# Seven half-depth products for 18 of the 52 pairs of weight chunks in a two-layer hybrid attention trunk

## The chip, the cores and the metric

The kernel runs on one core of one Trainium2 chip. The metric is device time in microseconds; lower is better. Five engines work side by side, each in the order of its own instruction queue: PE multiplies matrices, DVE (VectorE), ACT (ScalarE) and POOL (GpSimd) work elementwise, and SP only starts transfers. ACT and POOL have queues for transfers as well. On-chip memory is SBUF; PE writes its results to eight banks of PSUM.

## The reference

Two layers work on x of 256 tokens by 2048 channels, all in float32. Each layer does this:

```python
h = rms_norm(x, norm_gain)
proj = jnp.einsum('bsd,de->bse', h, w_in)          # 2048 -> 20480, ten segments of 2048
(da_q, da_k, da_v, da_z, sb_q, sb_k, sb_v, sb_z, gate_a, gate_b) = split_columns(proj)
...                                                # da_q, da_k: rms_norm per head, rope
oa = differential_attention(...)                   # softmax(q1 k1) - lam * softmax(q2 k2), times v
ua = rms_norm(oa, subln_gain) * (1.0 - lambda_init) * silu(da_z)
ub = stick_breaking_attention(qs, ks, vs) * silu(sb_z)
y = sigmoid(gate_a) * (ua @ w_branch_a) + sigmoid(gate_b) * (ub @ w_branch_b)
x = x + y @ w_out
```

So a layer multiplies 256 tokens with thirteen weight matrices of 2048 by 2048: ten segments of w_in, two branch projections and one output projection. Both attentions are causal, with 128-token query blocks.

## The kernel before

A **chunk** is 512 columns of such a matrix, so each matrix has four chunks and a layer has 52; the two layers together have 52 pairs of chunks. A chunk arrives from DRAM as eight tiles of 128 x 1024 float32 (512 KB): each holds two of its 16 depth tiles of 128 rows.

PE takes its operands in a reduced float32 format. To keep precision, each operand is split in two: a high part `h` (ACT copies it into the reduced format) and a rest `l` (DVE subtracts `h` from the source). `split` in L61 and L62 does that for every weight tile (`wraw` into `wh` and `wl`) and for every activation. `mm3` in L65 to L67 then adds three matmuls into one PSUM bank: high by high, high by rest, rest by high. Each has 512 columns for a weight chunk.

`project` multiplies one chunk: for eight weight tiles, two depth tiles each, two token tiles and three matmuls, 96 matmuls in all, into two of the four PSUM banks of the pool `ps_mm`. With four banks, the next chunk can start while the last one is still being read out. `load_w` loads a weight tile on SP's queue (four `wraw` buffers) and splits it (three buffers each for `wh` and `wl`).

A layer goes through four groups of differential attention and then four of stick-breaking attention. A group is four chunks (q, k, v, z) with the attention of its heads: `da_qk` normalises per head and applies rope (squares on ACT, the root by `rsqrt_mean` on POOL, the rest on DVE and POOL), `put_T` transposes on PE and splits, `scores` and `attn_T` make the weights, `v_proj` and `act_proj` read their PSUM banks with the scale of the layer's input norm. That scale is applied after the projection: x goes in only multiplied by `norm_gain`, transposed (from the host for layer 0), and each result is multiplied with 1/rms of its token. So the first projection can begin while the sums of squares are still being made.

The branch results `ua` and `ub` stay in SBUF, split. In the merge, the gates are projected, then `w_a` from `ua` and `w_b` from `ub`; then the output projection follows. In layer 0, each finished output chunk is stored, multiplied with the next gain, transposed and split for layer 1.

The text of the program is not the order of the engines: a scheduler that plans with priorities (weight splits are raised by 400) arranges each engine's queue when the kernel is built. Buffers are handed out from pools; an instruction that needs a taken buffer waits for its last reader.

Of the kernel before, what the change touches and what calls it, by code (L numbers as in the profile page):

```python
# [9 lines left out]
F32 = mybir.dt.float32  # L10
# [22 lines left out]
QK_SCALE = HD ** -0.5  # L33

# [4 lines left out]
def trunk(ctx: ExitStack, tc: tile.TileContext, x, xT, gT, norm_gain, w_in, qk_gain, lam_vecs,  # L39
# [19 lines left out]

    def split(h, l, src):  # L60
        nc.scalar.copy(h, src)  # L61
        nc.vector.tensor_tensor(out=l, in0=src, in1=h.bitcast(F32), op=ALU.subtract)  # L62

    def mm3(ps, lh, ll, rh, rl, start, stop):
        nc.tensor.matmul(ps, lhsT=lh, rhs=rh, start=start, stop=False)  # L65
        nc.tensor.matmul(ps, lhsT=lh, rhs=rl, start=False, stop=False)  # L66
        nc.tensor.matmul(ps, lhsT=ll, rhs=rh, start=False, stop=stop)  # L67
# [5 lines left out]
    gcol = const.tile([P, KT], F32, name="gcol")  # L73
    nc.scalar.dma_start(out=gcol, in_=gT)

    def load_w(src, parts=1, between=None):
        raw = wp.tile([P, KK * CW], F32, name="wraw", bufs=4)
        h = wp.tile([P, KK * CW], F32R, name="wh")
        l = wp.tile([P, KK * CW], F32R, name="wl")
        n = KK * CW // parts  # L80
        for i in range(parts):
            c = slice(i * n, (i + 1) * n)
            nc.sync.dma_start(out=raw[:, c], in_=src[:, c])  # L83
            if between is not None and i == 0:
                between()
            with tc.high_priority(offset=400):
                split(h[:, c], l[:, c], raw[:, c])
        return h, l

    def project(src, lhs, before=None):  # L90
        ps = [ps_mm.tile([P, CW], F32, name="mm") for _ in range(NT)]
        for kp in range(KP):
            if before is not None and kp == 0:
                h, l = load_w(src[kp], KK, lambda: before(0))
            else:
                if before is not None:
                    before(kp)
                h, l = load_w(src[kp])
# [8 lines left out]
        return ps  # L107

    def pair(tag):
        return (big.tile([P, KT, S], F32R, name=tag + "h", tag=tag + "h"),  # L110
                big.tile([P, KT, S], F32R, name=tag + "l", tag=tag + "l"))

    def put_T(src, dst, c, t):
        """Four 128x128 blocks of src, transposed and split, into k-tiles 4c.. of dst."""
        tr = ps_tr.tile([P, CW], F32, name="tr")
# [4 lines left out]
        trv = heads(tr)  # L120
        split(dst[0][:, js, ts], dst[1][:, js, ts], trv)

    def rsqrt_mean(ss, n):
        """(ss / n + eps) ** -0.5"""
# [7 lines left out]

# [1 line left out]
    xt = pair("xT")  # L134
    ss_part = small.tile([P, NT, NG], F32, name="ss_part", bufs=2)
    sq_junk = const.tile([P, CW], F32, name="sq_junk")

    def first_input(kp):
        raw = work.tile([P, CW], F32, name="tok")
        if kp:  # L140
            nc.sync.dma_start(out=raw, in_=xT[:, kp * CW:(kp + 1) * CW])  # L141
        for j in range(KK):
            k = kp * KK + j
            rv = raw[:, j * S:(j + 1) * S]
            if kp:
# [36 lines left out]
    for l in range(DEPTH):  # L182
# [303 lines left out]
        if not last:  # L486
            xt = xt_n
            x_in = x_next
# [50 lines left out]
```

## Time and profile before

| what | value |
|---|---|
| median of three runs | 2439.18 us (2438.13 to 2440.94) |
| span of the profiled execution | 2436.2 us |
| PE busy | 2427.0 us, 11328 matmuls and transposes |
| DVE busy | 1430.3 us |
| ACT busy | 1257.7 us |
| POOL busy | 179.7 us |
| DMA, mean over the span | 186 GB/s, 453 MB |
| clock granted to PE | full, all through |

The profiled execution's span is 3.0 us below the median of the runs. In rows that list groups of instructions, the name to the left of `<-` is the tile that is written, those to the right are read; then come the shapes, the count, the busy time in us and the mean length of one instruction in ns, and last the idle time ahead of it with the engine that ended it. A matmul's length in such a row includes its way through the array; the next one starts earlier, so its cost in a stream is the distance between starts. The same holds, less strongly, for DVE. In the rows of a timeline the first number is the start in us from the beginning of the span, the second the length.

### The profile page before, as it was taken

What the parts mean: (1) busy time and instruction counts of PE and PEld (TensorE: products, weight loads), DVE (VectorE), ACT (ScalarE), POOL (GpSimd) and SP (SyncE); (2) the same over time, 40 slices, a digit from 0 to 9 for tenths busy, and PEclk for the clock granted to TensorE, in tenths of its full rate; (3) what the DMA queues carried; (4) which work ended last, traced back from release to release, by engine and by line L of the source; (5) the groups of instructions that cost most, each with busy time, mean ns of one, the idle gap of its engine ahead of it and who ended that gap; (6) DMA issues with size and microseconds to landing.
All of it is one profiled execution on the core that took longest, in us unless ns stands there. A gap on an engine that the chain in (4) does not pass through costs nothing.

```text
span 2436.2 us, 29977 instructions
## 1 busy us (share of the span) xinstructions
PE 2427.0 (100%) x11328; PEld 2019.4 (83%) x11328; DVE 1430.3 (59%) x1636; ACT 1257.7 (52%) x1771; POOL 179.7 (7%) x183
## 2 busy tenths in 40 slices
PE   9999999999999999999999999999999999999999
PEld 7888888888888888888888888888888888888887
DVE  7676766655656444555566757656556564445554
ACT  6555655645645444444455555556556454444443
POOL 2031130000000000000030321300000000000000
PEclk9999999999999999999999999999999999999999
DMA  8555555555555555556755555555555555555565
GB/s 291 170 174 179 173 179 179 175 176 171 172 179 174 196 191 195 191 192 201 240 199 173 176 179 173 173 182 173 173 174 173 182 173 192 196 191 191 189 206 182
DMA packets 128386, 453.39 MB, mean 186 GB/s; under 512 B 14321, under 2 KB 15089, under 8 KB 128241
## 3 DMA queue, kind: packets, MB, share of 16 engines
q1 hardware_dynamic: 127312, 449.24, 55.5%
q8 instruction: 89, 1.46, 0.3%
q0 software_dynamic: 640, 2.10, 0.2%
q14 instruction: 57, 0.46, 0.1%
q10 hardware_dynamic: 288, 0.14, 0.0%
HBM read 447.23 MB, written 4.19 MB: 185 GB/s over the span
## 4 chain that ended last, share of the span: by engine, by line
PE 99%; DMA 0%; SPq 0%; DVE 0%; ACT 0%; issue 0%; DVEq 0%
PE mm L66 31%; PE mm L67 31%; PE mm L65 31%; PE tr L117 2%; PE sc L67 1%; PE sc L66 1%; PE sc L65 1%; PE tr L323 1%; PE tr L415 0%; DMA wraw<-in_w_in 0%; DVE wl L62 0%; ACT wh L61 0%; SPq L148 0%; SPq L83 0%; SPq L141 0%; DVE tok L473 0%
## 5 line engine op out<-in xcount | busy, mean ns | idle before, releaser
L62 DVE TENSOR_TENSOR wl<-wraw,wh 128x1024 fp32r<-128x1024 f32 (+1 forms) x833 | 1026.3, 1232 | 838.1 <-ACT wh L61 837.5
L61 ACT CAST wh<-wraw 128x1024 fp32r<-128x1024 f32 (+1 forms) x833 | 875.7, 1051 | 969.8 <-PE mm L67 946.0
L66 PE MATMUL mm<-wl,xTh 128*128 128x512 f32 x2560 | 1004.6, 392 | 0.5 <-DVE wl L62 0.5
L67 PE MATMUL mm<-wh,xTl 128*128 128x512 f32 x2560 | 1004.6, 392 | 0.0
L65 PE MATMUL mm<-wh,xTh 128*128 128x512 f32 x2560 | 930.4, 392 | 4.6 <-DVE xTh L149 4.4
L65 PEld LDWEIGHTS mm<-wh,xTh 128*128 128x128 f32 x2560 | 480.5, 188 | 101.7 <-ACT wh L61 5.3
L66 PEld LDWEIGHTS mm<-wl,xTh 128*128 128x128 f32 x2560 | 481.5, 188 | 96.7 <-DVE wl L62 1.1
L67 PEld LDWEIGHTS mm<-wh,xTl 128*128 128x128 f32 x2560 | 481.5, 188 | 95.4
L66 PE MATMUL mm<-wl,uah 128*128 128x512 f32 x512 | 199.6, 390 | 0.0
L67 PE MATMUL mm<-wh,ual 128*128 128x512 f32 x512 | 199.3, 389 | 0.0
L65 PE MATMUL mm<-wh,uah 128*128 128x512 f32 x512 | 180.1, 390 | 0.0
L65 PEld LDWEIGHTS mm<-wh,uah 128*128 128x128 f32 x512 | 96.1, 188 | 19.9
L67 PEld LDWEIGHTS mm<-wh,ual 128*128 128x128 f32 x512 | 96.1, 188 | 19.8
L66 PEld LDWEIGHTS mm<-wl,uah 128*128 128x128 f32 x512 | 96.1, 188 | 19.7
L66 PE MATMUL mm<-wl,ubh 128*128 128x512 f32 x256 | 99.6, 389 | 0.0
L67 PE MATMUL mm<-wh,ubl 128*128 128x512 f32 x256 | 99.6, 389 | 0.0
L65 PE MATMUL mm<-wh,ubh 128*128 128x512 f32 x256 | 89.2, 389 | 0.0
L480 POOL DMA_DIRECT2D x_next<-tok x8 | 4.5, 567 | 828.8 <-DVE tok L473 828.8
L127 POOL TENSOR_SCALAR rv<-ssq 128x4 f32<-128x4 f32 (+1 forms) x48 | 26.7, 556 | 523.7 <-ACT sq_junk L372 272.5
L117 PEld LDWEIGHTS tr<-ident,tok 128*128 128x128 f32 x416 | 51.2, 140 | 12.5
L117 PE MATMUL tr<-ident,tok 128*128 128x128 f32 x416 | 60.9, 272 | 0.0
L130 POOL TENSOR_TENSOR rr<-rv,mhalf 128x4 f32<-128x4 f32 (+1 forms) x50 | 57.9, 1157 | 4.2
(115 smaller groups left out, 1524.8 us busy)
## 6 DMA issues: line engine op xcount, KB each, us to landing
wraw<-in_w_in SPq DMA_DIRECT2D x639, 512.0 KB, 3.3
wraw<-in_w_a SPq DMA_DIRECT2D x64, 512.0 KB, 3.3
wraw<-in_w_b SPq DMA_DIRECT2D x64, 512.0 KB, 3.3
wraw<-in_w_o SPq DMA_DIRECT2D x64, 512.0 KB, 3.9
tok<-in_x SPq DMA_DIRECT2D x8, 256.0 KB, 6.8
xr<-in_x SPq DMA_DIRECT2D x4, 512.0 KB, 5.6
x_next<-tok POOLq DMA_DIRECT2D x8, 256.0 KB, 5.2
xr<-x_next SPq DMA_DIRECT2D x4, 512.0 KB, 5.4
```

Of the source, the lines that this page charges most:

```text
L61: nc.scalar.copy(h, src)
L62: nc.vector.tensor_tensor(out=l, in0=src, in1=h.bitcast(F32), op=ALU.subtract)
L65: nc.tensor.matmul(ps, lhsT=lh, rhs=rh, start=start, stop=False)
L66: nc.tensor.matmul(ps, lhsT=lh, rhs=rl, start=False, stop=False)
L67: nc.tensor.matmul(ps, lhsT=ll, rhs=rh, start=False, stop=stop)
L117: nc.tensor.transpose(out=tr[:, j * P:(j + 1) * P], in_=src[:, j * P:(j + 1) * P], identity=ident)
L127: nc.gpsimd.tensor_scalar(out=v[:, :w], in0=ss, scalar1=1.0 / n, scalar2=RMS_EPS, op0=ALU.mult, op1=ALU.add)
L130: nc.gpsimd.tensor_tensor(out=r[:, :w], in0=v[:, :w], in1=mhalf[:, :w], op=ALU.pow)
L323: nc.tensor.transpose(out=tr[:, j:j + P], in_=a[:, j:j + P], identity=ident)
L480: nc.gpsimd.dma_start(out=x_next[t * P:(t + 1) * P, cs], in_=xn)
```

## The change

**Seven products.** Two weight chunks with the same left-hand side, side by side, form a right-hand matrix of 2048 by 1024. Cut in halves both ways, it has the blocks b11, b21 (the upper and lower half of the first chunk's depth) and b12, b22 (of the second chunk's). The left-hand side (the 256 normalised tokens) has four blocks as well: two token tiles by two halves of the depth. The eight block products become seven, in Winograd's arrangement of Strassen's method, each of half the depth (8 depth tiles) for one token tile: 7 x 8 x 3 = 168 matmuls, where two chunks took 192. `s_stream` does this. Four sums of left-hand blocks (`sm`, made and split once per layer by `left_sums`) replace some left-hand blocks; sums of right-hand blocks are made in place in the raw tiles. These sums are of three kinds: "a" adds b12 to b11, "c" adds b12 to the remainder, "d" adds b21; all three are transfers from DRAM that POOL issues and that add to what lies in SBUF (`accum_op=ALU.add`). "b" adds two raw tiles on DVE. In the gate pair "d" is also done on DVE, so that there are 12 such transfers in 16 of the pairs and 8 in two. Each of the 28 right-hand tiles of the seven products is split anew. The four result tiles come from five combinations on DVE, which read PSUM and held copies (`pp`, three of them made by ACT).

In each layer the pairs are v and z of all eight groups, and the second chunks of the two gates: 9 pairs per layer, 18 in all. All other chunks are multiplied as before (`c_stream`). `run` interleaves two such streams by their share of steps: beside a group's seven products go the q and k chunks of the next group, each followed by two empty steps (`GAP`).

**PSUM.** Two banks for `c_stream` (`mc`), three for the seven products (`sU`, `sN`, `sQ`), three for transposes, scores and attention results (`at`). Where no seven products run, successive chunks take turns between `mc` and `sU`/`sN`.

**Input normalised first.** x is loaded, squared, scaled with 1/rms and the gain, transposed and split before the first projection of a layer, in both layers (`normalised`). The scaling of the results disappears from the read-out.

**Branches in DRAM.** Each group's `ua` or `ub` part goes to DRAM (`spill`, on POOL's queue) and comes back before the merge (`reload`), since the sums `sm` take its place in SBUF. Raw tiles have ten buffers instead of four.

```diff
+RAW = 10
+PPB = 5
+GAP = 2
...
-    ps_mm = ctx.enter_context(tc.tile_pool(name="ps_mm", bufs=4, space=PSUM))
-    ps_tr = ctx.enter_context(tc.tile_pool(name="ps_tr", bufs=2, space=PSUM))
-    ps_sc = ctx.enter_context(tc.tile_pool(name="ps_sc", bufs=2, space=PSUM))
+    ps_c = ctx.enter_context(tc.tile_pool(name="ps_c", bufs=2, space=PSUM))
+    ps_s = ctx.enter_context(tc.tile_pool(name="ps_s", bufs=1, space=PSUM))
+    ps_at = ctx.enter_context(tc.tile_pool(name="ps_at", bufs=3, space=PSUM))
...
+        def add(dst, src, dma_src, key):
+            with tc.high_priority(offset=400):
+                if key in by_dma:
+                    nc.gpsimd.dma_start(out=dst, in_=dma_src, accum_op=ALU.add)
+                else:
+                    nc.vector.tensor_tensor(out=dst, in0=dst, in1=src, op=ALU.add)
+
+        def prod(ps, lhs, get, after=None, more=False):
+            for i in range(hk):
+                raw = get(i)
+                h, l = split_raw(raw)
+                for kk in range(KK):
+                    k = i * KK + kk
+                    cs = slice(kk * CW, (kk + 1) * CW)
+                    mm3(ps, lhs[0][:, k], lhs[1][:, k], h[:, cs], l[:, cs],
+                        k == 0 and not more, k == KT // 2 - 1, more)
+                if after is not None:
+                    after(i)
+                if i < hk - 1:
+                    yield
...
+        u_ps = ps_s.tile([P, CW], F32, name="sU")
+        yield from prod(u_ps, a(0, 0), loader(xs, b11), lambda i: add(xs[i], None, b12[i], "a"))
+        p1 = held("p1")
+        nc.scalar.copy(p1, u_ps)
+        yield
+
+        n_ps = ps_s.tile([P, CW], F32, name="sN")
+        yield from prod(n_ps, s(3), loader(zs, b22))
+        yield
+
+
+        def after5(i):
+            add(xs[i], zs[i], b22[i], "b")
+            add(zs[i], None, b12[i], "c")
+
+        q_ps = ps_s.tile([P, CW], F32, name="sQ")
+        yield from prod(q_ps, s(0), lambda i: xs[i], after5)
+        p5 = held("p5")
+        nc.scalar.copy(p5, q_ps)
+        yield
+
+        yield from prod(u_ps, s(1), lambda i: xs[i],
+                        (lambda i: add(xs[i], None, b21[i], "d")) if "d" in by_dma else None, True)
+        w = held("w")
+        nc.vector.tensor_tensor(out=w, in0=u_ps, in1=p5, op=ALU.subtract)
+        u = held("u")
+        nc.scalar.copy(u, u_ps)
+        fin(1, 0, lambda dst: nc.vector.tensor_tensor(out=dst, in0=n_ps, in1=w, op=ALU.subtract))
...
+        v_ps = ps_s.tile([P, CW], F32, name="sQ")
+        yield from prod(v_ps, s(2), lambda i: zs[i])
...
+        r_ps = ps_s.tile([P, CW], F32, name="sN")
+        yield from prod(r_ps, a(1, 0), loader(ws, b21),
+                        None if "d" in by_dma else (lambda i: add(xs[i], ws[i], None, "d")))
...
+        yield from prod(v_ps, a(1, 1), lambda i: xs[i], None, True)
...
+            s = s_stream(w_chunk(bases[0], g), w_chunk(bases[1], g), xt, sm,
+                         lambda col, t, op: cols[col](t, op), "acd")
+            if n + 1 < 2 * NG:
+                c = qk_streams(n + 1, gap=GAP)
...
+            run((2 * (C_STEPS + GAP), c), (S_STEPS, s))
...
+            nc.gpsimd.dma_start(out=xk[c], in_=x_in[:, cs].rearrange("(t p) d -> p t d", p=P))
+            run((1, c_stream([w_o[l, c, kp] for kp in range(KP)], yT, o_fin(c), c % 2 == 1)))
         if not last:
-            xt = xt_n
+            xt = normalised(xk, gb, ss_part)
```

How this moves the queues shows at three places.

On PE, in a differential-attention group of layer 0 before, where one chunk ends (banks 904 and 905) and the next begins (banks 1071 and 1072), without anything between:

```order
L65 MATMUL mm_905<-wh_1033,xTh_87 128x512
L66 MATMUL mm_905<-wl_1034,xTh_87 128x512
L67 MATMUL mm_905<-wh_1033,xTl_88 128x512
L65 MATMUL mm_1071<-wh_1074,xTh_87 128x512
L66 MATMUL mm_1071<-wl_1075,xTh_87 128x512
```

The same engine in the change, where a q chunk ends (bank 815 is its second token tile): transposes and scores (`at`) follow, then matmuls of the third product (`sQ`).

```order
L74 MATMUL mc_815<-wh_1059,xTl_132 128x512
L458 MATMUL at_766<-ident_85,tok_763 128x128 x2
L72 MATMUL at_771<-kTh_589,qTh_391 128x256
L73 MATMUL at_771<-kTl_590,qTh_391 128x256
L74 MATMUL at_771<-kTh_589,qTl_392 128x256
```

The k chunk's first matmul (`mc_1186`) comes 45 rows later, after the rest of the third product and the whole fourth.

On POOL, before, in the first differential-attention group: root (`rv`, `rr`) and rope (`tok`) of the k chunk.

```order
L127 TENSOR_SCALAR rv<-ssq 128x4
L130 TENSOR_TENSOR rr<-rv,mhalf 128x4
L260 TENSOR_TENSOR tok<-tok,t_k 128x4x64
L262 TENSOR_TENSOR tok<-tok,t_k 128x4x64
L127 TENSOR_SCALAR rv<-ssq 128x4
```

The change, at the same place, with the accumulating transfers into raw tiles between them:

```order
L141 DMA raw<-in_w_in 128x1024
L247 TENSOR_SCALAR rv<-ssq 128x4
L250 TENSOR_TENSOR rr<-rv,mhalf 128x4
L141 DMA raw<-in_w_in 128x1024
L404 TENSOR_TENSOR tok<-tok,t_k 128x4x64
L406 TENSOR_TENSOR tok<-tok,t_k 128x4x64
```

The second root of the chunk now stands behind transfers that wait for DVE's split of their tile.

On DVE, in a differential-attention group before, at the read-out of a q chunk (`mm`) with rope behind it:

```order
L62 TENSOR_TENSOR wl<-wraw,wh 128x1024 x6
L246 TENSOR_SCALAR cf<-rr,rstd_s 128x4
L250 TENSOR_TENSOR tok<-mm,cf 128x512
L62 TENSOR_TENSOR wl<-wraw,wh 128x1024
L257 TENSOR_TENSOR tok<-tok,t_q 128x512
L264 TENSOR_TENSOR tok<-tok 128x512
```

In the change, during the third product: "b" additions (L143) and softmax steps between the splits.

```order
L68 TENSOR_TENSOR wl<-raw,wh 128x1024
L143 TENSOR_TENSOR raw<-raw 128x1024
L480 RECIPROCAL rs<-sums 128x2
L68 TENSOR_TENSOR wl<-raw,wh 128x1024
L482 TENSOR_SCALAR nrs<-rs,nlam 128x2
L68 TENSOR_TENSOR wl<-raw,wh 128x1024
L143 TENSOR_TENSOR raw<-raw 128x1024
```

Where splits stood in runs of up to six, each split at this place is now followed by another DVE instruction.

More of the change, by code (lines that the diff above doesn't have):

```diff
@@ new lines, in trunk, with run, chain, slot @@
+    C_STEPS, S_STEPS = KP, 7 * KP // 2
+    def run(*streams):
+        live = [[n, 0, g] for n, g in streams]
+        while live:
+            s = min(live, key=lambda s: (s[1] + 0.5) / s[0])
+            if next(s[2], "end") == "end":
+                live.remove(s)
+            s[1] += 1
+    def chain(*gens):
+        for g in gens:
+            yield from g
+    def slot(tag, name):
+        return (big.tile([P, KT, S], F32R, name=name + "h", tag=tag + "h"),
+                big.tile([P, KT, S], F32R, name=name + "l", tag=tag + "l"))
@@ L169, in trunk @@
     nc.gpsimd.memset(mhalf, -0.5)
+    ss_part = small.tile([P, NT, NG], F32, name="ss_part", bufs=2)
+    xk = []
+    for c in range(NG):
+        xc = chunk_tile(c, "xk")
+        for t in range(NT):
+            nc.sync.dma_start(out=xc[:, t], in_=x[t * P:(t + 1) * P, c * CW:(c + 1) * CW])
+        xk.append(xc)
+    gb = gains(0)
+    for c in range(NG):
+        for t in range(NT):
+            squares(xk, c, t, ss_part)
+    xt = normalised(xk, gb, ss_part)
     masks = {}
```

525 lines of the change are left out of this document (310 added, 215 removed).

## The prediction

> **What bounds the kernel now.** I read the page's totals first, then the chain that ended last, then the busy time by stage.
>
> ```profile
> PE 2427.0 (100%) x11328; PEld 2019.4 (83%) x11328; DVE 1430.3 (59%) x1636; ACT 1257.7 (52%) x1771; POOL 179.7 (7%) x183
> PE 99%; DMA 0%; SPq 0%; DVE 0%; ACT 0%; issue 0%; DVEq 0%
> 0.00:45.00 45.00, 39.84 (x164) 32.04 (x165) 30.79 (x51) 32.64 (x65) 7.83 (x19) 1.00 0.91 328
> 45.00:330.00 285.00, 285.00 (x1361) 237.59 (x1360) 196.06 (x257) 162.00 (x308) 65.31 (x62) 1.00 0.53 175
> 420.00:800.00 380.00, 380.00 (x1834) 317.71 (x1833) 219.16 (x245) 211.43 (x255) 0.00 (x0) 1.00 0.53 175
> 840.00:1020.00 180.00, 180.00 (x800) 149.10 (x799) 87.96 (x78) 75.94 (x78) 0.00 (x0) 1.00 0.57 193
> ```
>
> The chain is PE from end to end. In the windows (start:end, length, then busy PE, PEld, DVE, ACT, POOL, then clock, DMA share, GB/s) PE is idle only at the start. 45 to 330 us holds three differential-attention groups, 95.0 us each, with DVE busy 65.4 us in each (69%); 420 to 800 us holds four stick-breaking groups, again 95.0 us, DVE 54.8 us. So matmuls taken away are worth their full spacing, until DVE, which splits every weight tile, or the DMA queues become the limit.
>
> **What the change takes away.** A pair of chunks is 192 matmuls of 512 columns; the seven products need 7 x 8 x 3 = 168. Eighteen pairs save 432.
>
> ```profile
> 118.04 0.39 PE L67 MATMUL mm<-wh,xTl 128*128 128x512 f32 x1
> 122.57 0.39 PE L67 MATMUL mm<-wh,xTl 128*128 128x512 f32 x1
> ```
>
> Between these two starts lie 20 spacings: 0.2265 us each. 432 x 0.2265 = **-97.8 us**. Shapes and operand types stay, so I keep the spacing. A group loses 24 matmuls: 95.0 - 5.4 = 89.6 us of PE.
>
> **What it adds on PE.** Layer 0's input is now transposed on the chip, 32 transposes.
>
> ```profile
> 1002.75 1.04 PE L117 MATMUL tr<-ident,tok 128*128 128x128 f32 x8
> 1003.54 0.48 PE L66 MATMUL mm<-wl,xTh 128*128 128x512 f32 x1
> ```
>
> Eight take 0.79 us up to the next start, 32 take **+3**.
>
> **Start.** Normalising first puts the whole of x, eight squares, the root and one transposed tile ahead of the first projection.
>
> ```profile
> 4.43 1.19 PE L65 MATMUL mm<-wh,xTh 128*128 128x512 f32 x2 [4.43 <-DVE xTh L149]
> tok<-in_x SPq DMA_DIRECT2D x8, 256.0 KB, 6.8
> L484 ACT ACTIVATE sq_junk<-tok 128x512 f32<-128x512 f32 x8 | 5.0, 628 | 0.1
> L484 ACT ACTIVATION_READ_ACCUMULATOR sq_junk<-tok 128x1 f32 x8 | 1.5, 186 | 0.0
> L130 POOL TENSOR_TENSOR rr<-rv,mhalf 128x2 f32<-128x2 f32 x18 | 12.6, 699 | 1.5
> L482 DVE TENSOR_TENSOR tok<-tok 128x512 f32<-128x512 f32 x8 | 5.5, 688 | 0.1
> L61 ACT CAST xTh<-tr 128x512 fp32r<-128x512 f32 x8 | 4.7, 583 | 3.8 <-PE tr L117 3.8
> ```
>
> Eight loads of 256 KB at the 328 GB/s of the first window take 6.4 us; with 3 us ahead of the first byte's use they are in at about 10. The last square ends 0.8 us later, reduction and root take 1.3 with hand-overs, then scale 0.69, transposes 0.4, cast 0.58: first matmul near 14 us. Today's start loses 45 - 164 x 0.2265 = 7.9 us, so +6. Then DVE is short: from the new order, with the spacing found below, the first 45 us of PE work carry 50 us of DVE work (splits, scaling, rope, the four left-hand sums). +4. Together **+10** (from 5, if DVE gets ahead while PE waits, to 16).
>
> **Layer boundary.** Before, the next layer's tiles were transposed chunk by chunk under the output projection. Now PE waits from the last output matmul through add 0.69, square 0.81, root 1.0, scale 0.69, transposes 0.4, cast 0.58, by the same rows: 4.2 and some 0.8 of hand-overs, then the same DVE shortage of 4. **+9** (5 to 14).
>
> **The splits.** Seven products split 28 right-hand tiles where 16 were split: 12 more casts on ACT, 12 more subtractions on DVE per pair, and four additions of 128x1024 on DVE.
>
> ```profile
> 142.39 1.22 DVE L62 TENSOR_TENSOR wl<-wraw,wh 128x1024 fp32r<-128x1024 f32 x1
> 143.52 0.68 DVE L62 TENSOR_TENSOR qTl<-tr,qTh 128x512 fp32r<-128x512 f32 x1
> 144.12 1.22 DVE L62 TENSOR_TENSOR wl<-wraw,wh 128x1024 fp32r<-128x1024 f32 x1
> 137.66 1.76 DVE L62 TENSOR_TENSOR wl<-wraw,wh 128x1024 fp32r<-128x1024 f32 x1
> 138.29 1.72 POOL L262 TENSOR_TENSOR tok<-tok,t_q 128x256 f32<-128x256 f32 x1
> ```
>
> Back to back, 1024 columns occupy DVE 1.13 us and 512 columns 0.60. So a group gains 16 x 1.13 + five combinations x 0.60 - four small cf operations x 0.23 = 20.2 us of DVE: 65.4 becomes 85.6 of 89.6 in differential attention (96%), 54.8 becomes about 76 in stick-breaking (85%). The gate pairs have almost only splits, 44 x 1.13 + 8 x 1.13 + 3 = 62 us beside 82. ACT gains 12 casts and copies, about 15 us on 54: no limit.
>
> PE need not wait by the sum alone. But DVE runs in order, only three wl buffers let it work ahead, and rope and softmax steps come in clusters. The last two rows show a subtraction stretched from 1.22 to 1.76 us while POOL ran beside it; 14 more POOL transfers per group (12 accumulating, 2 storing), each stretching one, would add 14 x 0.54 = 7.6 us: 93.2 against 89.6, and at 95% of DVE filled 98 us. So a differential-attention group costs between 0 and 8.4 us of waiting; nothing in the rows excludes either, and I take the middle, 4. The other ten stages lie between 0 (85% or less, as PE today meets 69% with no wait) and 3 (7.6 us more would bring 76 to 84 of 89.6); 1. 8 x 4 + 10 x 1 = **+42**.
>
> The Trainium skill, page "SBUF — State Buffer", section "Who interferes with whom", says that a DVE instruction with two SBUF inputs and a GpSimd instruction that reads SBUF exclude each other; the 1.76 us row agrees. [...]
>
> **One PSUM pair for the attention chunks.** With two banks instead of four, the next q or k chunk waits until the last is read out.
>
> ```profile
> 124.58 0.37 ACT L241 ACTIVATE sq_junk<-mm,rstd 128x128 f32<-128x128 f32 x1 [0.53 <-PE mm L67]
> 129.72 0.69 DVE L250 TENSOR_TENSOR tok<-mm,cf 128x512 f32<-128x512 f32 x1
> 136.32 0.69 DVE L250 TENSOR_TENSOR tok<-mm,cf 128x512 f32<-128x512 f32 x1
> ```
>
> From the first square, the first bank is free after 5.8 us and the second after 12.4, because POOL does the first tile's rope ahead of the second's root. In the new order the work between a bank's last and next use comes to 10.5 and 13.7 us at q to k, but 6.8 and 10.2 at k to the next q (matmuls counted, times 0.2265). The second bank may be 1 to 2 us late, three times per layer: inside the 4 above. On POOL each accumulating transfer waits for the DVE split of its tile, and in the new order the roots and rope steps of the same group, which free these banks, stand behind such transfers; a late split then holds a bank too. That makes the waits of a group hang together and is why I do not add them.
>
> **DMA.**
>
> ```profile
> wraw<-in_w_in SPq DMA_DIRECT2D x639, 512.0 KB, 3.3
> x_next<-tok POOLq DMA_DIRECT2D x8, 256.0 KB, 5.2
> ```
>
> A group issues 28 plain loads, 12 accumulating transfers of 512 KB and 2 stores. At 53% of 95 us for 32 loads, a load holds the 16 DMA engines for 1.57 us. 30 plain ones take 47 us of 89.6, leaving 42.5: the accumulating ones fit up to 3.5 us each, 2.25 loads. No row shows one. Below, it costs a plain load, 1.57; above, nothing in the trace bounds it, except that an in-place add reads two operands for one. Each result is wanted one or two products (13 to 26 us) after its issue, against 5.2 us of landing. I take **0**, and leave the rest to a rival. The reload of both branches lies under two chunks (43.5 us) and four (87 us): 0.
>
> The Trainium skill, page "Collectives: The Full Stack", section "The bandwidth ceiling: the fold count and why AG ≠ RS ≠ AR", holds that an add in the DMA path costs two source reads and so halves the rate. By it the group's DMA work would be 47 + 12 x 3.14 = 85 of 89.6 us: still hidden, with no slack. No run here shows it yet.
>
> **Sum.** 2436.2 - 97.8 + 3 + 10 + 9 + 42 = 2402 for a profiled execution. The median of the runs lies 3.0 above the profiled span (2439.18 to 2436.2), so **2405 us**, 1.4% faster.
>
> **Rivals.** *A, all is hidden.* For it: PE met DVE at 69% without a wait, and the order interleaves the streams. Against: 96% is another matter. Without the 42: 2363. *B, DVE is the limit in differential attention.* At 98 us per group, 8.4 x 8 = 67 and ten times 2 = 20 instead of 42: 2450 at the worst, 2440 where only the first holds and the rest is 1: no change. For it the 1.76 row, against it that POOL's transfers hold POOL for only 0.54 us. *C, the accumulating transfers are the limit, slower.* Place: products 3 to 5 of a group, where eight or more are issued and only two of the ten raw buffers are left for the other stream. The price decides from the point where a group takes 47 + 12 x p = 94 us instead of 92, p = 3.9 us (2.5 loads): the gain is gone. At 3 loads it is 104 us a group, 16 x 12 = +190, near 2595; at 2.6, 96 us, 2470. For it: twelve half-megabyte read-modify-writes per group in a stage with 53% already used. Against: a rate even halved fits.
>
> **How the numbers follow.** Forecast (2380 to 2430) 0.45, A 0.22, B 0.13, C 0.20. Within 0.2% (2434 to 2444, about what a measurement tells from no change) lies a third of B and a little of C: 0.06. Faster: forecast, A and a third of B, 0.71. Slower: the rest, 0.23. The range 2355 to 2465 takes in A's floor, the forecast, B and the beginning of C; beyond lie most of C and little else.
>
> **What would show it.** Right: first matmul near 14 us, PE spacing still 0.227, a PE gap near 5 us at the boundary, DVE above 90% busy in differential attention, PE's idle time there released by wl subtractions. A shows as PE at 99%; B as PE idle 8 us per group, all released by DVE; C as DMA share above 0.95 and splits or POOL waiting for raw tiles. It would be wrong throughout if the spacing of the matmuls changed, or if PE waited on a bank for more than 2 us at each switch.

## The result and the profile after

The changed kernel takes **2498.87 us** (median, 2496.48 to 2501.29), the one before 2438.65: a ratio of 1.0245, 95% interval 1.023 to 1.0259. It is 2.4% slower. The forecast was 2405 with a range to 2465; the time is 94 us above the forecast and outside the range.

First the page of the changed kernel: engine totals, chain, transfer queues and the median landing times of weight loads and accumulating transfers.

```profile
PE 2390.2 (96%) x10928; PEld 1950.8 (78%) x10928; DVE 1829.2 (73%) x2065; ACT 1485.9 (60%) x2056; POOL 389.8 (16%) x463
PE 74%; DVE 13%; issue 4%; ACT 3%; DMA 3%; POOL 1%; DVEq 0%; ACTq 0%; POOLq 0%
q1 hardware_dynamic: 111744, 402.57, 48.0%
q0 software_dynamic: 40960, 148.92, 28.9%
raw<-in_w_in SPq DMA_DIRECT2D x568, 512.0 KB, 4.8
raw<-in_w_in POOLq DMA_DIRECT2D x208, 512.0 KB, 7.3
```

The matmul count is the expected one, 11328 - 432 + 32 = 10928, but the chain, which was 99% PE, now runs 13% over DVE and 11% over the others. Now the windows of the changed kernel (start:end, length, busy PE, PEld, DVE, ACT, POOL, clock, DMA share, GB/s).

```profile
0.00:25.00 25.00, 6.81 (x22) 5.04 (x23) 9.77 (x15) 11.99 (x24) 2.62 (x13) 1.00 0.92 345
96.09:396.14 300.05, 284.89 (x1305) 228.24 (x1304) 253.26 (x306) 197.21 (x344) 87.38 (x102) 0.98 0.81 220
329.90:333.40 3.50, 3.33 (x12) 2.73 (x13) 2.15 (x4) 1.68 (x5) 2.68 (x4) 0.77 1.05 275
517.10:807.66 290.56, 278.64 (x1325) 229.40 (x1323) 224.93 (x247) 194.46 (x235) 35.54 (x43) 0.99 0.85 229
```

PE is busy 6.81 us of the first 25. The second row holds three differential-attention groups: **100.0 us each**, where 95.0 were before and 93.6 were forecast. The last holds three stick-breaking groups: **96.9 us** against 95.0 before and 90.6 forecast. From here on these two windows, cut at the same matmuls (start of the 332nd record to that of the 1636th, and of the 2178th to that of the 3501st), are the yardstick of the runs with products; I call them DA and SB. DVE's work per group is as forecast (84.4 and 75.0 us; forecast 85.6 and 76). What it does to PE is not.

The PE timeline in a DA group shows where the time goes (start, duration, instruction, idle time before it and what ended it).

```profile
216.31 0.50 PE L73 MATMUL sU<-wl,smh 128*128 128x512 f32 x1 [1.09 <-DVE wl L68]
...
316.92 0.50 PE L73 MATMUL sU<-wl,smh 128*128 128x512 f32 x1 [1.06 <-DVE wl L68]
323.48 0.50 PE L73 MATMUL sU<-wl,smh 128*128 128x512 f32 x1 [1.17 <-DVE wl L68]
326.05 0.50 PE L72 MATMUL sQ<-wh,smh 128*128 128x512 f32 x1 [1.14 <-ACT wh L67]
327.61 0.50 PE L73 MATMUL sQ<-wl,smh 128*128 128x512 f32 x1 [0.64 <-DVE wl L68]
330.07 0.76 PE L72 MATMUL mc<-wh,xTh 128*128 128x512 f32 x1 [0.36 <-DVE tok L394]
```

Five waits fall into 14 us around the fourth and fifth products, four of them for splits and none long; the same instruction waits again one group (100.6 us) earlier. DVE's timeline at the same place, first and last row of a stretch without a gap:

```profile
311.97 1.22 DVE L68 TENSOR_TENSOR wl<-raw,wh 128x1024 fp32r<-128x1024 f32 x1
...
324.47 0.16 DVE L480 RECIPROCAL rs<-sums 128x2 f32<-128x2 f32 x1
```

For 12.7 us DVE goes from split to addition to softmax step. The chain in an SB group shows another mechanism (start, length, piece).

```profile
522.02 1.14 DVE wl L68
...
523.18 9.28 DMA raw<-in_w_in
...
532.56 1.05 ACT wh L67
...
533.63 1.24 DVE wl L68
```

A load of the other stream goes out only at 523.18, when a split has freed a raw tile, and lands 9.28 us later.

PE also ran slower behind its waits: the mean granted clock was 0.989 (1.000 before), and the row 329.90:333.40 has 0.77 just behind them. The matmuls that start at 328.22, 328.65 and 329.07 us lie 0.43 apart instead of 0.23, so I count such spells as half speed. Together they last about (1 - 0.989) x 2496 / 0.5 = 55 us; that is an estimate, and it makes them at most 27 us of the loss.

### The profile page after: what moved, and what is told of

It reads as the page before. It is cut to its first block, busy times and chain, and to the rows that moved or that the text cites. A ratio compares the mean times of both kernels' runs of the same rounds, so it can differ in the third digit from the quotient of the medians.

```text
span 2496.3 us, 30730 instructions
## 1 busy us (share of the span) xinstructions
PE 2390.2 (96%) x10928; PEld 1950.8 (78%) x10928; DVE 1829.2 (73%) x2065; ACT 1485.9 (60%) x2056; POOL 389.8 (16%) x463
## 3 DMA queue, kind: packets, MB, share of 16 engines
q0 software_dynamic: 40960, 148.92, 28.9%
## 4 chain that ended last, share of the span: by engine, by line
PE 74%; DVE 13%; issue 4%; ACT 3%; DMA 3%; POOL 1%; DVEq 0%; ACTq 0%; POOLq 0%
PE mc L73 13%; PE mc L74 13%; PE mc L72 13%; DVE wl L68 7%; PE sN L72 4%; PE sN L73 4%; PE sN L74 4%; PE sU L73 4%; PE sU L74 4%; PE sU L72 4%; DMA raw<-in_w_in 2%; PE sQ L73 2%; PE sQ L74 2%; PE sQ L72 2%; DVE raw L143 2%
## 5 line engine op out<-in xcount | busy, mean ns | idle before, releaser
L68 DVE TENSOR_TENSOR wl<-raw,wh 128x1024 fp32r<-128x1024 f32 x1048 | 1278.1, 1229 | 556.2 <-ACT wh L67 537.1
L67 ACT CAST wh<-raw 128x1024 fp32r<-128x1024 f32 x1048 | 1097.6, 1051 | 884.5 <-PE mc L74 369.0
L73 PE MATMUL mc<-wl,xTh 128*128 128x512 f32 x1280 | 505.9, 395 | 9.2 <-DVE wl L68 9.0
L74 PE MATMUL mc<-wh,xTl 128*128 128x512 f32 x1280 | 503.5, 394 | 0.0
L72 PE MATMUL mc<-wh,xTh 128*128 128x512 f32 x1280 | 471.3, 398 | 13.6 <-ACT wh L67 10.3
L141 POOL DMA_DIRECT2D raw<-in_w_in x208 | 181.0, 874 | 941.0 <-DVE wl L68 263.0
L72 PEld LDWEIGHTS mc<-wh,xTh 128*128 128x128 f32 x1280 | 241.1, 191 | 72.0 <-ACT wh L67 14.7
L73 PEld LDWEIGHTS mc<-wl,xTh 128*128 128x128 f32 x1280 | 242.9, 190 | 66.7 <-DVE wl L68 17.7
L74 PEld LDWEIGHTS mc<-wh,xTl 128*128 128x128 f32 x1280 | 242.5, 190 | 49.2
L72 PE MATMUL sQ<-wh,smh 128*128 128x512 f32 x288 | 115.2, 400 | 7.3 <-ACT wh L67 7.3
L73 PE MATMUL sQ<-wl,smh 128*128 128x512 f32 x288 | 114.8, 399 | 2.1 <-DVE wl L68 2.0
L143 DVE TENSOR_TENSOR raw<-raw 128x1024 f32<-128x1024 f32 x80 | 97.4, 1221 | 5.9 <-DMA raw<-in_w_in 5.8
L73 PE MATMUL sU<-wl,xTh 128*128 128x512 f32 x208 | 83.4, 401 | 10.3 <-DVE wl L68 10.0
L73 PE MATMUL sU<-wl,smh 128*128 128x512 f32 x144 | 63.4, 440 | 27.0 <-DVE wl L68 27.0
L72 PE MATMUL sU<-wh,xTh 128*128 128x512 f32 x208 | 81.9, 394 | 0.8 <-ACT wh L67 0.8
L73 PE MATMUL sN<-wl,xTh 128*128 128x512 f32 x208 | 81.7, 393 | 0.0
L72 PE MATMUL sN<-wh,xTh 128*128 128x512 f32 x208 | 81.2, 390 | 0.0
```

What stands on the lines that cost most here:

```text
L141: nc.gpsimd.dma_start(out=dst, in_=dma_src, accum_op=ALU.add)
L143: nc.vector.tensor_tensor(out=dst, in0=dst, in1=src, op=ALU.add)
```

## The experiments

Theory D: DVE's additions and splits starve PE. T: the accumulating transfers make weight loads late. K: the single pair of banks for the attention chunks is read out too late. Times are medians; the kernel before took 2438.5 to 2439.3 beside them.

### The price of the accumulating transfers, and the additions

```diff
# e1_plain
-                    nc.gpsimd.dma_start(out=dst, in_=dma_src, accum_op=ALU.add)
+                    nc.gpsimd.dma_start(out=dst, in_=dma_src)
# e2_no_b   (e7_neither: both)
+                if key == "b":
+                    return
```

> The 208 accumulating transfers are made plain loads of the same 512 KB from the same queue, so the sums of right-hand blocks are left out; instructions, waits and order stay as in the changed kernel. Theory D (the vector engine's clusters set the end: four additions and twelve more splits per pair): nothing but the transfers changes, so within 8 us of 2499. Theory T (the accumulating transfers hold the DMA engines for about 2.9 us each against 1.5 for a plain load, and loads come late): the DMA share in a group falls from about 0.83 to about 0.65, the late loads at the start and the end of the stick-breaking groups go (5 us of idle time each, twelve such groups and gate stages), and the run comes to 2430 to 2460. Theory K (the two banks of the attention chunks are read out too late): within 5 us of 2499.

> The four additions of 128x1024 on the vector engine in each of the 18 pairs are left out (72 of the 80 rows of that form, 1.22 us each and 1.13 back to back; the other 8 belong to the gate pairs' last sum), so these blocks are not summed. Theory D: the waits for wl in products 3 and 4 go (about 4 of the 7.4 us of idle time in a differential-attention group, and the half-speed spells after them), 18 x 3 to 18 x 4.5 us less, 2420 to 2445. Theory T: the accumulating transfers stay, so the stick-breaking groups keep their 97 us; 2475 to 2495. Theory K: 2490 to 2500, since the read-out of the banks goes over the scalar and GpSimd engines.

> Both of the first two edits together: the 208 accumulating transfers are plain loads, and the four additions on the vector engine per pair are left out. Alone they brought 23.3 and 21.9 us. If the two costs are separate stalls (theories D and T both hold, side by side): 2499 - 45 = 2454, within 5. If one stall has two causes that cover for each other: 2462 to 2475. If they feed each other (a late addition makes a transfer late that makes a split late): below 2447.

Measured: **2475.56**, **2476.97** and **2439.98** us. Alone, neither remedy brings what its own theory asked (T below 2460, D below 2445); together they bring 59, more than 23 + 22, so the two costs feed each other. Windows of e1_plain, DA ahead of SB:

```profile
96.57:398.11 301.54, 284.85 (x1306) 228.76 (x1304) 253.50 (x306) 197.30 (x344) 78.27 (x102) 0.98 0.65 219
516.82:797.35 280.53, 275.32 (x1324) 228.68 (x1322) 224.89 (x247) 195.24 (x235) 23.27 (x43) 1.00 0.71 238
```

The page of e1_plain, software queue and landing time:

```profile
q0 software_dynamic: 40960, 148.92, 17.9%
...
raw<-in_w_in POOLq DMA_DIRECT2D x208, 512.0 KB, 4.6
```

The windows of e2_no_b:

```profile
96.04:389.47 293.43, 280.79 (x1305) 226.06 (x1304) 241.86 (x294) 195.49 (x344) 90.33 (x103) 1.00 0.82 225
508.49:792.98 284.49, 277.04 (x1325) 228.09 (x1323) 211.69 (x234) 194.40 (x236) 34.59 (x42) 1.00 0.86 233
```

The stages separate the theories. The transfers' price costs SB 10 us per three groups and DA nothing; the additions cost DA 6.6 and SB 6.1. The software queue falls from 28.9% of 2496.3 to 17.9% of 2474.3 us: (721.4 - 442.9) / 208 = 1.34 us per accumulating transfer on top of the 1.57 of a plain load, so about 2.9 us, 1.85 loads.

### How many raw buffers

```diff
# e12_raw9
-RAW = 10
+RAW = 9
# e13_raw11: RAW = 11, PPB = 4, work tiles 5 instead of 6
```

> Nine raw weight buffers instead of ten; eight are held by a pair in products 3 to 5, so the other stream has one instead of two. Theory T (the loads of the other stream are issued late, because a buffer comes free late, and then land late): every group loses more, at least 3 us in 16 groups, above 2545. Theory D (vector engine alone): within 10 us of 2499, since its work is unchanged.

> Eleven raw buffers; the space comes from one of the five holding tiles of the products (four are live at most) and one of six work tiles. Theory T: the other stream has three buffers, its loads go out a product earlier, the late loads at the start of the stick-breaking groups go: 2455 to 2485. Theory D: 2494 to 2504. If the missing work tile costs more than the buffer brings, above 2504, and then the run tells nothing on T.

Measured: **2655.59** with nine, 2498.87 with ten, **2470.32** with eleven. ACT's waits for weight loads (total us, times, longest) in e12_raw9:

```profile
ACT wh L67 <- DMA raw<-in_w_in: 284.0, 84, 10.1
```

In the changed kernel:

```profile
ACT wh L67 <- DMA raw<-in_w_in: 48.3, 23, 5.9
```

In e13_raw11:

```profile
ACT wh L67 <- DMA raw<-in_w_in: 7.7, 8, 2.1
```

And the SB window of e13_raw11:

```profile
514.59:795.14 280.55, 275.33 (x1325) 228.74 (x1323) 225.01 (x247) 195.36 (x235) 35.54 (x43) 1.00 0.86 237
```

Theory T holds for SB, in this form: a load goes out late for want of a buffer. DVE's work is unchanged, the DMA share is 0.86 and yet SB falls to 280.55 us, just what the plain transfers brought. The transfers were not too many; the loads were too late.

> Eleven raw buffers (2470) and plain loads in place of the accumulating ones. Theory T in the form 'the buffer lets a load go out in time, the price makes it land late': both remedy the same stall, so beside 2470 the price now brings little, 0 to 8 us: 2462 to 2470. If the price also counts where no buffer is short: again 20 or more, below 2450.

```diff
# f1_raw11_plain: e13_raw11 with the edit of e1_plain
```

Measured: **2464.29**. With eleven buffers the price of an accumulating transfer matters by some 6 us instead of 23: one stall with two remedies.

> Whole computation kept: in the eight stick-breaking pairs the last sum (four tiles) is added on the vector engine instead of by accumulating transfers, as in the gate pairs; 32 of 208 accumulating transfers go, 32 additions of 128x1024 (1.13 us back to back) come. By the queue shares an accumulating transfer takes 2.9 us of the 16 engines, so such a group's transfers fall from about 83% to about 72% of its time, and its vector engine's work rises from about 75 to 79.5 of 97 us. Theory T (loads late behind the accumulating burst): 2 to 4 us less per stick-breaking group, 2467 to 2483. Theory D: 0 to 2 us more per group, 2499 to 2515.

> Whole computation kept: eleven raw buffers (2470), and the last sum of the eight stick-breaking pairs on the vector engine. With ten buffers that brought 10 us. Theory T: the stick-breaking groups lose almost nothing more to late loads with eleven buffers, so 0 to 3 us: 2467 to 2472. If the transfers' total matters: about 2460.

```diff
-                         lambda col, t, op: cols[col](t, op), "acd")
+                         lambda col, t, op: cols[col](t, op), "acd" if da else "ac")
```

Measured: **2488.73** with ten buffers, **2474.01** with eleven. Fewer transfers bring 10 us only as long as a buffer is short. With eleven the move brings nothing; the 4 us more are 0.15%, about what runs of one kernel differ by.

### The additions of the third product

```diff
# f3_raw11_no_b: e13_raw11 with the edit of e2_no_b
# e14_b_on_pool (ten buffers)
+                    eng = nc.gpsimd if key == "b" else nc.vector
+                    eng.tensor_tensor(out=dst, in0=dst, in1=src, op=ALU.add)
# g1_da_b_by_dma: f5_raw11_sb_d_dve with "abcd" in differential attention
```

> Eleven raw buffers (2470), the four vector additions per pair left out. Theory D: in differential attention the three waits of 1.1 to 1.4 us near the splits of products 3 and 4 go, eight groups, 30 us or more with the half-speed spells: below 2445. If those additions cost only because a raw buffer came free later: 2460 to 2470.

> Whole computation kept: the four additions of product 3 are made by GpSimd instead of the vector engine. From its rows (128x256 in 1.2 and 0.7 us) one takes 2.9 to 4.7 us there, 12 to 19 us a pair. If only the vector engine's own work counts (theory D): as with the additions left out, 2475 to 2485. If the two engines stretch each other (a subtraction took 1.76 instead of 1.22 us beside a GpSimd row), and since each sum now comes later and the accumulating transfers of the pair stand behind it on GpSimd: above 2520.

> Whole computation kept: as the run beside it, and in the eight differential-attention pairs the additions of product 3 are accumulating transfers too, so that the vector engine makes none there. Vector work per group falls by 4.5 us, transfers rise from 30 x 1.56 + 12 x 2.9 = 82 to 94 us of about 99. Theory D (vector additions are what starves the matmuls in these groups, price of a transfer hidden): 15 to 25 us less than its neighbour, 2440 to 2455. If the DMA engines become the limit (94 us filled at 95% is 99): 2465 to 2500.

Measured: **2436.18**, **2556.37** and **2475.57**. DA window of e13_raw11:

```profile
94.62:394.05 299.43, 283.60 (x1306) 227.42 (x1304) 252.54 (x306) 197.24 (x344) 88.79 (x102) 0.99 0.81 220
```

Of f3_raw11_no_b:

```profile
96.02:387.92 291.90, 279.82 (x1305) 226.22 (x1304) 242.45 (x294) 195.98 (x344) 90.62 (x103) 1.00 0.83 226
```

Of g1_da_b_by_dma:

```profile
94.68:395.53 300.85, 282.22 (x1306) 226.04 (x1304) 242.76 (x294) 195.88 (x344) 101.01 (x115) 1.00 0.90 241
```

The eleventh buffer does nothing for DA (299.43 against 300.05); leaving the additions out does (291.90), so theory D holds there. But it is not DVE's total alone: in g1 DVE is busy as little as in f3 (242.8 and 242.5 us) and the groups are as long as with the additions on DVE. Product 4 follows product 3 at once on the same tiles, so whoever makes the sum stands between two splits of one tile. In g1 the wait moved to the transfers: in its DA window ACT's casts wait six times for a raw tile to land, 11.1 us together, and in that of e13 not once. PE waits 9.9 us there for the splits of product 4 (L73 into `sU`), 9.1 in e13 and 5.7 in f3. On GpSimd, where an addition took 2.94 us, the whole is 57 us slower, as that expectation's second case has it: beside these additions DVE's own instructions took longer (rows further below).

### What the products cost in all, and what the rest costs

```diff
# e8_no_resplit: add() returns at once; products 3, 4, 5 and 7 get None as raw tile
+                if raw is None:
+                    h, l = [sm[j][:, 0:2].rearrange("p a k s -> p (a k s)") for j in range(2)]
+                else:
+                    h, l = split_raw(raw)
# e4_no_products: s_stream becomes two plain c_streams (banks sU, sN), no left_sums
# f2_plain_4banks: e4 with ps_c of 4 banks and ps_at of 2
# e10_plain_roots: e4 with the edit of e9_roots_first (below)
```

> All additions and accumulating transfers of the products left out, and the four products that multiply summed or reused blocks (3, 4, 5 and 7) take two ready tiles of the left-hand sums as their right side, so 16 of 28 splits per pair and their casts fall away too; all matmuls, loads, banks and the interleaving of the products stay. If the splits and additions are all that the products cost beside their matmuls: the plain variant (2500) less 97.8, near 2402. If the interleaving of seven short products with the other stream, or the three banks they share, stalls the matmuls by itself: above 2420.

> The 18 pairs are multiplied plainly again (two chunks after each other in the second pair of banks, 32 loads, 32 splits, no additions, no left-hand sums); input normalised first, branch outputs through DRAM, bank layout and interleaving stay. Prediction of the matmul count: 97.8 us more of PE work than the changed kernel. If the stalls all belong to the products (theories D and T): the kernel before, plus 3 for transposes, plus start and boundary, 2439 + 15 to 25 = 2455 to 2465. Theory K, or stalls from storing and normalising: 2480 to 2520, with the waits at the q to k switches still there.

> The 18 pairs plain (2500), with four banks for the attention chunks instead of two (the products' third bank and one of the three transpose banks given to them). Theory K (61 us over the kernel before, of which some 36 are waits at the chunk switches of differential attention, the rest start and layer boundary): those go, 2462 to 2472. If fewer transpose banks or the scalar engine's order hold the matmuls instead: 2490 or more.

Measured: **2383.12**, **2500.00** and **2473.39**. The plain pairs in the new frame cost as much as the products: the frame with plain pairs is 61 us slower than the kernel before, and the products save 97.8 us of matmuls and lose as much. Windows of e8_no_resplit, DA ahead of SB:

```profile
94.97:375.32 280.35, 276.63 (x1306) 227.21 (x1306) 185.21 (x248) 151.69 (x305) 54.88 (x64) 1.00 0.51 169
488.71:759.69 270.98, 270.98 (x1324) 227.65 (x1323) 163.25 (x192) 154.04 (x193) 3.19 (x6) 1.00 0.53 175
```

With the second splits gone too, PE is busy throughout SB, 90.3 us a group, and the matmuls of the products run as forecast; seven short products and three banks are no obstacle there. A DA group still takes 93.5. (This variant makes 12 splits a pair, where the plain form makes 16, so it flatters the products.) The chain of e4_no_products at a k-to-q switch in differential attention, pieces of one read-out:

```profile
368.99 0.61 DVE tok L403
...
369.67 1.24 POOL tok L413
370.91 1.68 POOL tok L415
...
372.68 0.70 POOL rv L256
...
373.45 1.02 POOL rr L259
```

The second bank's root waits behind GpSimd's two rope steps of the first half, as theory K says. Four banks end this in the plain form: 2500.0 to 2473.4. What f2 keeps over the kernel before is 34 us. I give each matmul the median spacing of its width (0.227 us for 512 columns, 0.12 for 256, 0.11 for 128) and call the rest of a stretch lost: by this count about 16 us are the start, 8 the layer boundary, 4 the transposes, and the rest lies in the stages.

### Taking the bank wait out of the products' form

```diff
# e9_roots_first (e10_plain_roots: in the plain form)
+                    ns.append(nv)
+                for t in range(NT):
+                    nv = ns[t]
                     a = tok()
# e3_copy
+                cp = [tok() for _ in range(NT)]
+                with tc.high_priority(offset=400):
+                    for t in range(NT):
+                        nc.scalar.copy(cp[t], ps[t])
# squares, root and rope then read cp; 32 copies in all (the expectation says 64)
# f7_raw11_3banks: e13_raw11, ps_c 3 banks, ps_at 2
```

> In differential attention both banks of a q or k chunk are copied to SBUF by the scalar engine first, with the splits' priority, and squares, root and rope read the copy; 64 copies of 128x512 more on the scalar engine. Theory K: the matmuls no longer wait at q to k and k to q (2.5 us of idle time near 325 us and 1.4 near 369 us in each such group, with the half-speed spell behind it), 7 x 4 to 7 x 6 us less: 2455 to 2475. Theories D and T: within 8 us of 2499, either way, since the same vector work and transfers stay.

> Whole computation kept: in differential attention the roots and the scalings of both token halves come ahead of the rope steps of the first, so that the second bank is not read out behind GpSimd's two rope steps (1.2 and 0.7 us). Theory K: the 1.35 us wait at each k to q switch and part of the 2.4 us at q to k go, 13 switches, 15 to 30 us with the half-speed spells behind them: 2469 to 2484. If the second bank is not what the matmuls wait for: 2494 to 2504.

> The same reordering in the variant with 18 plain pairs (2500). There the trace shows 1.8 us of waiting at each k to the next q (behind GpSimd's rope steps), and 3.5 us at each q to k behind the gate's sigmoid-weighted activation and the squares on the scalar engine. Theory K: the first goes, 6 x 1.8 and little else: 2483 to 2491. If 2499 to 2502, the wait only moves to the vector or scalar engine.

> Whole computation kept: eleven raw buffers (2470), three banks for the attention chunks and two for transposes and scores. Theory K in the products' form: the 1.3 us at k to q and most of the 2.4 us at q to k go, 13 switches, 20 to 35 us with half-speed spells: 2435 to 2450. If the fewer transpose banks take it back, or the wait moves to the vector engine: 2465 to 2480.

Measured: **2537.99**, **2548.26**, **2509.91** and **2471.66**; none confirms K. Both e3 and e9 moved work in the queues so that a load of DA fell into the accumulating burst (10.51 us of landing on e3's chain). A piece of e9's chain, between accumulating transfers that GpSimd issues at 330.16 and 332.83 us:

```profile
331.12 9.46 DMA raw<-in_w_in
```

PE's longest wait behind it is 6.5 us. The DA window of e9:

```profile
98.89:413.41 314.52, 286.65 (x1305) 229.75 (x1304) 255.01 (x305) 199.03 (x352) 83.12 (x100) 0.96 0.78 209
```

In f7 the third bank came with eleven buffers, so without that effect, and at the price of a transpose bank; it brought nothing: PE's waits for wl at L73 of the other stream rose from 3.0 us (e13) to 14.7, by f7's waits of PE:

```profile
PE mc L73 <- DVE wl L68: 14.7, 27, 1.7
```

In the plain form the banks are the limit (f2); in the products' form a wait that goes at the banks comes back at the splits. In e10 the wait that it was aimed at did go (6.4 us of PE at L72 <- `tok` L403 in e4, none in e10), but PE's waits for casts, splits and the read-out of the other pair of banks grew. So a better order on GpSimd alone does not give the plain form its 27 us back. Why e10 was 10 us slower instead of 9 to 17 faster was not followed up.

## Why the prediction was wrong

**Ledger.** The medians step up from 2383 (matmuls of the products, no second splits, no sums) by 53 (16 splits per pair and the accumulating transfers; f3) to 2436, by 34 (four additions; e13) to 2470, and by 29 (the tenth instead of the eleventh buffer) to 2499. The forecast allowed 42 us over rival A's 2363 for all of this; it is 116, and 20 lie between 2363 and 2383. The sizes hold for this order of steps: with ten buffers the additions are 22. Of the 53, what an accumulating transfer costs over a plain one is little (6 in f1); the second splits and the 208 transfers as such were only left out together.

The two windows of three groups, in us, show where each step acts; three groups at the forecast's 89.6 would be 268.8.

| left out or changed | DA | SB |
|---|---|---|
| nothing (ten buffers) | 300.05 | 290.56 |
| eleventh buffer (e13) | 299.43 | 280.55 |
| and no additions (f3) | 291.90 | 275.69 |
| no second splits, no transfers (e8) | 280.35 | 270.98 |

**Matmuls, -97.8: right.** Count and spacing hold; behind waits the spacing nearly doubles in half-speed spells, which the forecast had no term for: at most 27 us, inside the steps above.

**Start, +10: too small.** The first projection starts at 18.97 us, not 14, by the PE timeline of the changed kernel:

```profile
16.49 2.82 PE L238 MATMUL at<-ident,tok 128*128 128x128 f32 x12 [16.49 <-DVE tok L279]
18.97 1.54 PE L72 MATMUL mc<-wh,xTh 128*128 128x512 f32 x2
```

The forecast let x's 2 MB have the DMA engines alone; the gain rows, 1 MB more, were under way at the same time. The squares waited for x up to the fourth of eight, at 10.7 us, and ended at 14.4 instead of 10.8. Counting the matmuls of the first 102 us at their spacing leaves 28 us lost, about 20 more than before. **Boundary, +9: nearly right**, about 12 by the same count. **Transposes, +3: right**, about 4.

**Stalls in the 18 stages, +42: the step that failed.** By the matmul count the stages lose 129 us, and lost 6 before: +123 where the sum has 42. Two steps of it were wrong. The first is the wait for splits, 4 us for a differential-attention group ("I take the middle, 4") and 1 for each other stage. DVE's load was forecast within 2%, but a load is no schedule. In DA the second splits, the additions and the softmax steps fall together; DVE runs without a gap from 311.97 to 324.6 us, and PE waits for splits behind it. A DA group takes 100.0 us where PE's forecast is 89.6: 10.4 over, more than rival B's ceiling of 8.4. An SB group is 7.3 over. The second is the DMA term ("I take **0**"): rival C named the right place, "only two of the ten raw buffers are left for the other stream", and the wrong condition. It looked for a price p at which the engines are full (3.9 us); at 2.9 and a share of 0.85 the loads already came too late in SB, and an eleventh buffer takes 29 us off the whole. The Trainium skill, page "Collectives: The Full Stack", section "The bandwidth ceiling: the fold count and why AG ≠ RS ≠ AR", was near on the price (3.14 estimated by its rule, 2.9 measured); what the forecast drew from it, "still hidden", was not.

**One PSUM pair, inside the 4: right here.** In the three DA groups PE waits only 1.6 us in all for the read-out of such a bank, and f7 gains nothing from a third one. It would have been wrong in the plain form, by 27 us.

**GpSimd stretching DVE: wrong for transfers, right for computing.** The forecast took one subtraction of 1.76 us as a sign that each POOL transfer stretches DVE by 0.54. POOL is busy for 210 us more than before, 181 of them issuing the accumulating transfers, and yet the subtractions take 1229 ns on average (the group of the changed kernel below), 1234 before.

```profile
L68 DVE TENSOR_TENSOR wl<-raw,wh 128x1024 fp32r<-128x1024 f32 x1048 | 1278.1, 1229 | 556.2 <-ACT wh L67 537.1 <-DMA raw<-in_w_in 3.0 <-DMA raw<-in_w_a 3.0
```

The 1.76 us row stood beside a rope step, not beside a transfer. Where GpSimd computes more, DVE does slow down. In e14, where GpSimd makes the 72 additions of 128x1024, the same subtractions take 1282 ns and a scan of stick-breaking attention 1294; in the changed kernel the scan takes 678.

```profile
L68 DVE TENSOR_TENSOR wl<-raw,wh 128x1024 fp32r<-128x1024 f32 x1048 | 1331.7, 1282 | 565.7 <-ACT wh L67 544.8 <-DMA raw<-in_w_in 4.5 <-DMA raw<-in_w_a 3.0
L558 DVE TENSOR_TENSOR_SCAN tok<-tok 128x256 f32<-128x256 f32 x32 | 40.2, 1294 | 5.0 <-ACT tok L552 5.0
```

**Verdict on the chances.** "Slower" had a chance of 0.23, most of it C's. C was right in place and wrong in its condition, B right in direction for half of the groups and too low there, and A, all hidden, did not come: 2363 is 136 us below the result. The forecast set each cost low within its bounds and judged B and C apart; parts of both came true in one run, and together they cost more than singly (59 against 45).

None of the runs that keep the whole computation beats the kernel before; the best, eleven buffers, is 28.5 us faster than the changed kernel and 1.24% slower than before (interval 1.04 to 1.44%).

## What to carry to other kernels

A saving of matmuls is worth its spacing only as far as every operand is ready: count how many instructions stand between two uses of the same tile, not only each engine's busy time, since DVE at 84% starved PE here. Where transfers and buffers are shared by two streams, ask how late a load can be issued and how long it then lands; one buffer more or less (2470, 2499, 2656 us) outweighed the price of the transfers. Before judging a change, run its frame without it: with plain pairs the frame cost 61 us, 27 of them for want of two banks, and putting the products in changed nothing either way.

## What the runs showed of the hardware

**DVE and GpSimd hold each other up, and a row of DVE instructions can hold GpSimd for its whole length.** GpSimd's timeline in the changed kernel's first 75 us, while the left-hand sums are made:

```profile
54.49 0.79 POOL L404 TENSOR_TENSOR tok<-tok,t_q 128x256 f32<-128x256 f32 x1 [0.86 <-PE sN L74]
...
65.42 7.75 POOL L404 TENSOR_TENSOR tok<-tok,t_q 128x256 f32<-128x256 f32 x1 [5.70 <-DVE tok L394]
```

DVE's timeline there, some rows of a stretch without a gap:

```profile
65.20 0.68 DVE L408 TENSOR_TENSOR tok<-tok 128x512 f32<-128x512 f32 x1
...
66.13 0.42 DVE L301 TENSOR_TENSOR raw<-raw 128x256 f32<-128x256 f32 x1
...
72.48 0.69 DVE L68 TENSOR_TENSOR qTl<-at,qTh 128x512 fp32r<-128x512 f32 x1
73.08 0.42 DVE L68 TENSOR_TENSOR sml<-raw,smh 128x256 fp32r<-128x256 f32 x1
```

The same rope step takes 0.79 us at 54.49 and 7.75 us at 65.42. In the first case DVE is held: its addition of 128x256 at 54.60 takes 0.96 us, where the one at 66.13 takes 0.42. In the second case GpSimd is held. From 65.20 on every DVE row has two operands in SBUF and its usual length (0.42 us, and 1.22 for the subtractions of 128x1024). The rope step ends at 73.17, together with the first row that reads a PSUM tile (`at`, at 72.48). In the second layer it is 7.75 us again, and it ends with the same row. The Trainium skill, page "SBUF — State Buffer", section "Who interferes with whom", says that a DVE instruction with two SBUF inputs and a GpSimd instruction that reads SBUF shut each other out for a whole instruction. Both cases agree; in the second, GpSimd was shut out over a whole row of such instructions.

**The granted clock fell behind short waits too.** In the changed kernel it fell behind several waits of 0.4 to 1.2 us within 14 us, none of them long (0.77 on average over the 3.5 us shown above). In the first DA group, where the waits at this place are shorter (five of 0.3 to 1.0 us within 8 us), it did not fall. That the waits lower the clock is inferred from this order; no run varied them alone.

**An accumulating transfer from DRAM into SBUF** held the DMA engines for about 2.9 us per 512 KB against 1.57 for a plain one, and landed in 7.3 us against 4.6 for a plain one in its place.
